# One layer of a hybrid decoder: output weights loaded ahead into other buffers and split by ScalarE and VectorE

## The chip, the cores and the metric

The kernel runs on one core of a Trainium2 chip. The metric is the device time of one execution in microseconds (us). Engines are named as in the profile: PE is TensorE (PEld its weight loads), DVE is VectorE, ACT is ScalarE, POOL is GpSimd, SP is the queue that issues most DMAs.

## The reference, cut to what matters

One layer (1024 positions, width 1024, float32). Both sub-layers have a residual; the lines around the change are:

```
p = modulate(rmsnorm(x)) @ w_in               # q, k, v (512 each) and u (512)
o_attn = stick_breaking(q, k, v)              # 8 heads of 64, in blocks of 128 queries
o_ssm  = s5(u)                                # state-space groups
o = concat([rmsnorm(o_attn, attn_out_g), rmsnorm(o_ssm, ssm_out_g)])
x = x + g1 * (o @ w_out)                      # g1 comes from c @ ada_w
x = x + g2 * ((gelu(gate) * val) @ w_down)    # val, gate: conv of modulate(rmsnorm(x)) @ w_up
```

In stick-breaking attention the weight of key s for query t is sigmoid(z) times the product of (1 - sigmoid(z)) over the keys between s and t, which the kernel forms by a scan along the keys.

## The kernel before

**Precision.** A float32 operand of a large matmul is split in two parts, hi (a rounded copy) and lo (raw minus hi), and each product is three matmuls: hi x hi, hi x lo, lo x hi.

**Stages.** After the norm, the state-space branch and the q and k projections comes the V projection (`proj` with chunk 2): eight tiles of 24 matmuls, three PSUM buffers; ACT and DVE turn each tile into `vt`, which SP writes to DRAM. Then come eight heads. For each tile of 128 queries `head` does: scores `z` on PE, two sigmoids on ACT (`nb`, `sig`), a scan over `nb` on DVE (line 736), a product on POOL into `sig` (line 738), transposes `wT` on PE, their split into `wh` (ACT) and `wl` (DVE), the products `ops` with the values on PE, and their sum into `oT`. Heads 0 to 5 run one after the other. Heads 6 and 7 run together, by groups of 256 queries from the last group (g = 3) to the first, and behind each group `tail_stats` takes the norm of `oT`.

**Output projection.** `w_out` is in eight blocks of 128 rows, k = 0 to 3 for attention (kind 0), 4 to 7 for the state-space half (kind 1). `wout_tile` (line 761) loads one block (`woraw`), scales it by the norm's gain and g1 in place on DVE (`stt`, line 766), rounds it on POOL (`wohi`) and subtracts on POOL (`wolo`). `woraw` has one buffer, tag `x1`, the same in which `ssm_out` accumulates a row tile. `wohi` and `wolo` have four buffers each, so attention's blocks take those of the state-space half. `ssm_out` loads a row tile of x, adds the state-space half's projection (`out_proj`, 24 matmuls `wops`) and writes it to DRAM (`x1_d`). `load_xacc` (line 859) brings those tiles back, two pairs into the `qkraw` buffers and four tiles into one buffer `xs`; `tail_proj` adds attention's half to them (24 matmuls a tile) and starts the second norm (transposes `tp`, line 986).

**Order.** `fillers` is a generator with 58 steps, and `marks` says at which share of the attention work each step is recorded; `ada_fill` does the same for the modulation rows (`ada_raw`, `adps`). A scheduler then fixes the order of instructions on each engine, and each engine runs its queue in that order. `act_copy` is a copy on ACT (line 174), `tt`, `ts` and `stt` are the helpers of lines 60 to 67, `pool_round` that of line 176.

Of the kernel before, what the change touches and what calls it, by code (L numbers as in the profile page):

```python
# [9 lines left out]
F32 = mybir.dt.float32  # L10
# [25 lines left out]
def hybrid_layer_kernel(  # L36
# [17 lines left out]
    act, dve, pool, pe, sp = nc.scalar, nc.vector, nc.gpsimd, nc.tensor, nc.sync  # L54

    def alloc(name, side="left", bufs=1, space=None):
        kw = {} if space is None else {"space": space}
        return tc.alloc_tile_pool(name=name, bufs=bufs, side=side, reuse_waits="tile", **kw)

    def tt(eng, out, a, b, op):  # L60
        eng.tensor_tensor(out=out, in0=a, in1=b, op=op)  # L61
# [4 lines left out]
    def stt(out, a, s, b, op0, op1):  # L66
        dve.scalar_tensor_tensor(out=out, in0=a, scalar=s, in1=b, op0=op0, op1=op1)  # L67

    MUL, ADD, SUB = ALU.mult, ALU.add, ALU.subtract
# [103 lines left out]
    def act_copy(o, i):  # L173
        act.activation(out=o, in_=i, func=AF.Copy)  # L174

    def pool_round(o, i):
        pool.tensor_scalar(out=o, in0=i, scalar1=1.0, scalar2=0.0, op0=MUL, op1=ADD)  # L177
# [37 lines left out]
    for k in range(NK):  # L215
# [4 lines left out]
        raw = ada_raw[k]  # L220
# [10 lines left out]
        hi = wp.tile([128, 512], F32R, tag="whi", name="wu_hi", bufs=8)  # L231
        lo = wp.tile([128, 512], F32R, tag="wlo", name="wu_lo", bufs=8)
# [165 lines left out]
    for i, (tab, k0) in enumerate(((rot[0], 0), (rot[1], 4))):  # L398
        pool.memset(tab[:, 0, :, 0:1], 1.0)
        pool.memset(tab[:, 1, :, 0:1], 0.0)  # L400
        for k in range(4 - i):
            n = 1 << k
# [218 lines left out]
    for cix in range(2):  # L621
        his, los = load_wchunk(cix)
        for tq in range(4):
# [14 lines left out]
            for j in range(2):  # L638
                t = tq * 2 + j
# [12 lines left out]
                for r in range(2):  # L652
                    act.dma_start(out=qk_d[cix, r].rearrange("(a p) t -> p a t", p=128)[:, :, t * 128:(t + 1) * 128],
                                 in_=hl[:, r].bitcast(F32).rearrange("p (a t) -> p a t", t=128))
    smb.release()
    sm.release()
    xq = alloc("qkraw", side="right")
    us = alloc("ffnmix", side="right")
    qp = alloc("qk", side="right")
    xs = alloc("ossm", side="right")  # L660

    def head_load_qk(hd):
        q1, q2, k1 = [qp.tile([128, 1024], F32R, tag=n_, name=n_, bufs=2) for n_ in ("q1", "q2", "k1")]
        for dst, w, sw in ((q1, 0, 0), (k1, 1, 0), (q2, 0, 1)):
            for r in range(2):
                sp.dma_start(out=dst[r * 64:r * 64 + 64].bitcast(F32), in_=qk_d[w, r ^ sw, hd * 64:hd * 64 + 64, :])
        return q1, q2, k1
# [21 lines left out]
    osp = alloc("oprep", side="right", bufs=2)  # L689
# [8 lines left out]
    def head_load_v(hd):  # L698
        vt = ap_.tile([128, 8, 128], F32R, tag="v", name="vsb")
        vload[0] = sp.dma_start(out=vt.bitcast(F32), in_=v_d.rearrange("(t p) h d -> p t h d", p=128)[:, :, hd, :])  # L700
        return vt

    def after_v(f, *a):
        with tc.issue_after(vlast.ins):
            return f(*a)
# [6 lines left out]
    def head(hd, stk, groups, after_tile, after_group):  # L712
        (q1, q2, k1), vt = stk
        pr, h = divmod(hd, 2)
        for g in groups:
# [42 lines left out]
            after_tile(2 * g + 1)  # L758
            after_group(g)

    def wout_tile(kind, kk, his, los):
        k = kind * 4 + kk
        raw = osp.tile([128, 1024], F32, tag="x1", name="woraw", bufs=1)
        sp.dma_start(out=raw, in_=w_out[k * 128:(k + 1) * 128, :])
        yield
        stt(raw, raw, outg_sb[:, k:k + 1], g1row, MUL, MUL)
        yield
        hi = wo.tile([128, 1024], F32R, tag="wohi", name="wohi", bufs=4)
        lo = wo.tile([128, 1024], F32R, tag="wolo", name="wolo", bufs=4)
        pool_round(hi, raw)  # L770
        tt(pool, lo, raw, hi.bitcast(F32), SUB)
        his.append(hi)
        los.append(lo)
        yield
# [40 lines left out]
    def run_all(gen):  # L815
        for _ in gen:
            pass

    psB_new = lambda nm: psM.tile([128, 512], F32, tag="mm", name=nm, bufs=MB)
    oS = xs.tile([128, 4, 8, 128], F32, tag="oS", name="oS")  # L820

    def ssm_stats(inv):
        after_v(lambda: sp.dma_start(out=oS, in_=o_d.rearrange("(k p) j c -> p k j c", p=128)))
        yield
        yield from mix_scale(ap_, psB_new("nps"), oS, range(NT), True, inv)
        yield

    def ssm_out(t, his, los, inv):
        xt_ = osp.tile([128, 1024], F32, tag="x1", name="x1", bufs=1)
        sp.dma_start(out=xt_, in_=x[t * 128:(t + 1) * 128, :])  # L830
        yield from out_proj(osp, psB_new, oS, t, True, his, los, xt_, inv)
        sp.dma_start(out=x1_d[t * 128:(t + 1) * 128, :], in_=xt_)

    def fillers():
        his, los = [], []
        inv = small.tile([128, NT], F32, tag="sinv", name="sinv", bufs=1)
        yield from wout_tile(1, 0, his, los)
        yield from wout_tile(1, 1, his, los)
        yield from ssm_stats(inv)
        yield from wout_tile(1, 2, his, los)  # L840
        yield from wout_tile(1, 3, his, los)
        for t in range(NT):
            yield from ssm_out(t, his, los, inv[:, t:t + 1])
        for kk in range(4):
            yield from wout_tile(0, kk, wa_hi, wa_lo)


    marks = [a + (b - a) * j / n for a, b, n in ((0.02, 0.13, 22), (0.13, 0.68, 24), (0.68, 0.75, 12)) for j in range(n)]
    wa_hi, wa_lo = [], []
    ada_fill = ada_back(ap_, ("adaw", "adacc", 2), psB_new, (c32b, mean32b), range(2, 8))  # L850
    ada_marks = [0.04 + 0.62 * j / 25 for j in range(25)]
    here = [None]
    fill = fillers()
    state = {"q": 0, "w": 0}

    n2inv = small.tile([128, NT], F32, tag="n2inv", name="n2inv", bufs=1)
    xacc = {}

    def load_xacc():
        for i in range(2):  # L860
            t_ = xq.tile([128, 2, 1024], F32, tag="qkraw", name=f"xq{i}", bufs=2)
            for j in range(2):
                xacc[2 - 2 * i + j] = t_[:, j, :]
        t_ = xs.tile([128, 4, 1024], F32, tag="oS", name="xs")
        for j in range(4):
            xacc[4 + j] = t_[:, j, :]
        for t in (6, 7, 4, 5, 2, 3, 0, 1):
            sp.dma_start(out=xacc[t], in_=x1_d[t * 128:(t + 1) * 128, :])

    tail = []  # L870
# [23 lines left out]
    for hd in range(NH):  # L894
        nxt = {}
        last_head = hd >= NH - 2

        def after_tile(i):
            if not last_head:
                if i == 0:  # L900
                    nxt["p"] = (after_v(head_load_qk, 1) if hd == 0 else head_load_qk(hd + 1), head_load_v(hd + 1))
            state["w"] += i + 2
            while ada_marks and ada_marks[0] <= state["w"] / (44.0 * NH):
                ada_marks.pop(0)
                with tc.issue_after(here[0].ins):
                    next(ada_fill, None)
            while state["q"] < len(marks) and marks[state["q"]] <= state["w"] / (44.0 * NH):
                state["q"] += 1
                with tc.issue_after(here[0].ins):
                    next(fill, None)  # L910

        if last_head:
            run_all(fill)
            run_all(ada_fill)
            load_xacc()
            stk2 = (head_load_qk(hd + 1), head_load_v(hd + 1))
            for g in (3, 2, 1, 0):
                head(hd, stk, (g,), after_tile, lambda g: None)
                head(hd + 1, stk2, (g,), after_tile, tail_stats)
            break  # L920
        head(hd, stk, range(4), after_tile, lambda g: None)
        stk = nxt.get("p")
# [280 lines left out]
    for n in range(2):  # L1203
# [15 lines left out]
        for t in range(NT):  # L1219
# [5 lines left out]
            t_ = dx.tile([128, 512], F32, tag="tmp", name="tmp", bufs=2)  # L1225
# [74 lines left out]
```

## Time and profile before

| | |
|---|---|
| median of three timed runs | 1316.16 us (1314.06 to 1320.03) |
| profiled execution | 1318.42 us, span 1316.6 us |
| PE busy, DVE busy | 1224.6 us (93%), 938.2 us (71%) |
| ACT busy, POOL busy | 600.9 us (46%), 460.1 us (35%) |
| mean granted clock of PE | 0.964 |

Times of single rows are us from the span's start. In the table of windows the figure of an engine is its busy time in that window, and `PEclk` the granted clock as a share of full speed. A wait names the instruction that waited, and behind the arrow what ended the wait. In a chain each row is a start, a duration and the work that the next row waited for.

### The profile page before, as it was taken

The page shows a single profiled execution, that of the slowest core. Times are in us where ns is not written, and L with a number is a line of the kernel's source. Part 1 is how long each engine was busy: PE and PEld are TensorE (multiplying, and loading weights), DVE is VectorE, ACT ScalarE, POOL GpSimd, SP SyncE. Part 2 cuts the span into 40 slices and gives each one's busy share as a digit, 9 for nine tenths or more (in the row PEclk, how much of TensorE's full clock was granted, in tenths as well). Part 3 has the DMA queues.
Part 4 walks back from the last instruction along what each step waited for, and adds up shares of the span by engine and source line. Part 5 has one row for each costly group of instructions (what it writes and reads, how often), then busy time and mean ns, then how long its engine had stood idle before and what let it go on. Part 6 is the DMA issues. An engine that isn't in the chain of part 4 may idle for free.

```text
span 1316.6 us, 17819 instructions
## 1 busy us (share of the span) xinstructions
PE 1224.6 (93%) x6384; PEld 994.2 (76%) x6384; DVE 938.2 (71%) x1443; ACT 600.9 (46%) x1039; POOL 460.1 (35%) x363
## 2 busy tenths in 40 slices
PE   5879989998889998769999999999999999999998
PEld 3668868886677767647877888888888888888887
DVE  4867788644897678858888888888888883345334
ACT  6431332423756566435664545545544553223220
POOL 4562370513763334540025545554554510000000
PEclk9988989999879998879999999999999999999999
DMA  9333454628757877214212222222222155447442
GB/s 382 143 84 95 113 167 99 144 89 254 211 144 209 256 195 191 96 64 137 72 48 89 73 96 81 88 72 96 73 80 89 65 191 185 144 168 248 150 137 105
DMA packets 147927, 178.43 MB, mean 136 GB/s; under 512 B 36208, under 2 KB 101888, under 8 KB 146816
## 3 DMA queue, kind: packets, MB, share of 16 engines
q1 hardware_dynamic: 127776, 157.38, 38.5%
q10 hardware_dynamic: 20064, 19.93, 4.4%
q8 instruction: 50, 0.82, 0.3%
q14 instruction: 37, 0.30, 0.1%
HBM read 135.19 MB, written 40.90 MB: 134 GB/s over the span
## 4 chain that ended last, share of the span: by engine, by line
PE 75%; DVE 12%; DMA 8%; issue 2%; ACT 1%; POOL 1%; SPq 0%; ACTq 0%; DVEq 0%; POOLq 0%
PE dnps L1209 6%; PE dnps L1210 6%; PE dnps L1211 6%; PE up_a L1031 6%; PE up_a L1032 6%; PE up_a L1030 6%; PE up_c L1032 3%; PE up_c L1031 3%; PE up_c L1030 3%; DMA ada_raw<-in_ada_r_dram 3%; PE qkvp L563 2%; PE qkvp L561 2%; PE qkvp L562 2%; PE wops L809 2%; PE wops L810 2%
## 5 line engine op out<-in xcount | busy, mean ns | idle before, releaser
L67 DVE SCALAR_TENSOR_TENSOR cv<-up,cols_sb,cv 128x1023 f32<-128x1023 f32 x88 | 147.5, 1677 | 20.5 <-ACT cv L1134 19.7
L61 DVE TENSOR_TENSOR alo<-araw,ahi 128x1024 fp32r<-128x1024 f32 x44 | 53.9, 1225 | 121.1 <-ACT ahi L174 121.0
L61 POOL TENSOR_TENSOR S<-upraw 128x512 f32<-128x512 f32 x40 | 76.0, 1901 | 181.5 <-DVE uplo L61 89.7
L1210 PE MATMUL dnps<-wdlo,ahi 128*128 128x512 f32 x352 | 136.9, 389 | 0.0
L1211 PE MATMUL dnps<-wdhi,alo 128*128 128x512 f32 x352 | 136.9, 389 | 0.0
L1209 PE MATMUL dnps<-wdhi,ahi 128*128 128x512 f32 x352 | 134.7, 389 | 0.0
L61 POOL TENSOR_TENSOR sig<-sig,nb 128x127 f32<-128x127 f32 (+3 forms) x64 | 91.4, 1437 | 97.3 <-DVE nb L736 52.8
L61 DVE TENSOR_TENSOR uplo<-S,uphi 128x512 fp32r<-128x512 f32 x80 | 97.2, 1216 | 27.7 <-ACT uphi L174 27.7
L174 ACT ACTIVATE ahi<-araw 128x1024 fp32r<-128x1024 f32 x44 | 46.6, 1060 | 148.5 <-PE dnps L1210 126.5
L736 DVE TENSOR_TENSOR_SCAN nb<-nb 128x128 f32<-128x128 f32 (+3 forms) x64 | 101.4, 1594 | 11.3 <-ACT nb L734 10.7
L61 POOL TENSOR_TENSOR cv<-cv 128x1024 f32<-128x1024 f32 x22 | 53.4, 2427 | 108.1 <-ACT cv L1138 96.9
L174 ACT ACTIVATE uphi<-S 128x512 fp32r<-128x512 f32 x80 | 49.8, 624 | 81.8 <-POOL S L61 67.6
L562 PE MATMUL qkvp<-w_lo,hhi 128*128 128x512 f32 x192 | 77.1, 402 | 0.0
L561 PE MATMUL qkvp<-w_hi,hhi 128*128 128x512 f32 x192 | 76.6, 402 | 0.0
L1211 PEld LDWEIGHTS dnps<-wdhi,alo 128*128 128x128 f32 x352 | 66.1, 188 | 13.8
L1209 PEld LDWEIGHTS dnps<-wdhi,ahi 128*128 128x128 f32 x352 | 66.1, 188 | 13.8
L1210 PEld LDWEIGHTS dnps<-wdlo,ahi 128*128 128x128 f32 x352 | 66.1, 188 | 13.6
L563 PE MATMUL qkvp<-w_hi,hlo 128*128 128x512 f32 x192 | 76.3, 399 | 0.0
L174 ACT ACTIVATE uphi<-upraw 128x512 fp32r<-128x512 f32 x68 | 42.9, 631 | 66.1 <-POOL cv L61 31.1
L61 DVE TENSOR_TENSOR uplo<-upraw,uphi 128x512 fp32r<-128x512 f32 x68 | 67.7, 996 | 1.5 <-ACT uphi L174 1.5
L1134 ACT ACTIVATE cv<-up,cols_sb 128x1024 f32<-128x1024 f32 x44 | 54.7, 1244 | 11.2 <-DVE up L61 10.4
L809 PE MATMUL wops<-wohi,ohi 128*128 128x512 f32 x128 | 53.4, 422 | 5.8 <-POOL wohi L177 3.8
(334 smaller groups left out, 3401.5 us busy)
## 6 DMA issues: line engine op xcount, KB each, us to landing
upraw<-in_w_up_dram SPq DMA_DIRECT2D x88, 256.0 KB, 3.4
araw<-a_d SPq DMA_DIRECT2D x44, 512.0 KB, 3.3
ada_raw<-in_ada_r_dram SPq DMA_DIRECT2D x64, 256.0 KB, 4.7
a_d<-cv ACTq DMA_DIRECT2D x22, 512.0 KB, 2.8
wdraw<-in_w_down_dram SPq DMA_DIRECT2D x44, 256.0 KB, 4.0
ada_raw<-in_ada_a_dram SPq DMA_DIRECT2D x8, 1024.0 KB, 6.0
qk_d<-hl ACTq DMA_DIRECT2D x32, 256.0 KB, 2.4
q<-qk_d SPq DMA_DIRECT2D x32, 256.0 KB, 7.0
```

What stands on the lines that cost most here:

```text
L61: eng.tensor_tensor(out=out, in0=a, in1=b, op=op)
L67: dve.scalar_tensor_tensor(out=out, in0=a, scalar=s, in1=b, op0=op0, op1=op1)
L174: act.activation(out=o, in_=i, func=AF.Copy)
L561: pe.matmul(o, lhsT=lh, rhs=his[k], start=(k == 0), stop=False)
L562: pe.matmul(o, lhsT=lh, rhs=los[k], start=False, stop=False)
L563: pe.matmul(o, lhsT=ll, rhs=his[k], start=False, stop=(k == NK - 1))
L1030: pe.matmul(ps, lhsT=hi[:, kt, :], rhs=rh, start=(first and kt == 0), stop=False, skip_group_check=True)
L1031: pe.matmul(ps, lhsT=hi[:, kt, :], rhs=rl, start=False, stop=False, skip_group_check=True)
L1032: pe.matmul(ps, lhsT=lo[:, kt, :], rhs=rh, start=False, stop=(kt == 3), skip_group_check=True)
L1209: pe.matmul(o[t], lhsT=hi[:, a], rhs=whi, start=(m == 0), stop=False)
L1210: pe.matmul(o[t], lhsT=hi[:, a], rhs=wlo, start=False, stop=False)
L1211: pe.matmul(o[t], lhsT=lo[:, a], rhs=whi, start=False, stop=(m == NM - 1))
```

## The change

1. Raw output weights no longer lie in the `x1` buffer. Two blocks at a time are loaded by one DMA of 1 MB into a `qkraw` buffer, of which there are two.
2. All eight blocks are rounded by ACT and subtracted by DVE.
3. Attention's four blocks are loaded and scaled among the first four tiles of `ssm_out`, and split behind the last.
4. The marks of the fillers are spread differently: the first 22 steps up to a share of 0.20 (before 0.13), the next 32 up to 0.70, the last 4 up to 0.74.
5. The two pairs of row tiles that come back into the `qkraw` buffers are loaded behind group 3 of head 6, the other four at the start of heads 6 and 7, behind the loads of head 7.

```diff
+    woraw = {}
     def wout_tile(kind, kk, his, los):
         k = kind * 4 + kk
-        raw = osp.tile([128, 1024], F32, tag="x1", name="woraw", bufs=1)
-        sp.dma_start(out=raw, in_=w_out[k * 128:(k + 1) * 128, :])
+        if kk % 2 == 0:
+            woraw[k // 2] = xq.tile([128, 2, 1024], F32, tag="qkraw", name="woraw", bufs=2)
+            sp.dma_start(out=woraw[k // 2], in_=w_out[k * 128:(k + 2) * 128, :].rearrange("(j p) n -> p j n", p=128))
+        raw = woraw[k // 2][:, kk % 2, :]
         yield
         stt(raw, raw, outg_sb[:, k:k + 1], g1row, MUL, MUL)
         yield
...
-        pool_round(hi, raw)
-        tt(pool, lo, raw, hi.bitcast(F32), SUB)
+        act_copy(hi, raw)
+        tt(dve, lo, raw, hi.bitcast(F32), SUB)
...
+        ahead = [wout_tile(0, kk, wa_hi, wa_lo) for kk in range(4)]
         for t in range(NT):
             yield from ssm_out(t, his, los, inv[:, t:t + 1])
-        for kk in range(4):
-            yield from wout_tile(0, kk, wa_hi, wa_lo)
+            if t < 4:
+                for _ in range(2):
+                    next(ahead[t])
+                    yield
+        for w_ in ahead:
+            yield from w_
-    marks = [... ((0.02, 0.13, 22), (0.13, 0.68, 24), (0.68, 0.75, 12)) ...]
+    marks = [... ((0.02, 0.20, 22), (0.20, 0.70, 32), (0.70, 0.74, 4)) ...]
...
-    def load_xacc():
-        for i in range(2):
+    def load_xacc(late_):
+        for i in range(2 * late_):
...
-            load_xacc()
             stk2 = (head_load_qk(hd + 1), head_load_v(hd + 1))
+            load_xacc(False)
             for g in (3, 2, 1, 0):
                 head(hd, stk, (g,), after_tile, lambda g: None)
+                if g == 3:
+                    load_xacc(True)
                 head(hd + 1, stk2, (g,), after_tile, tail_stats)
```

DVE's queue at the V projection, before (`vt` are the V subtractions, `nb` the scans of the first head):

```order
L61 TENSOR_TENSOR hl<-qkT,hl 128x512
L61 TENSOR_TENSOR vt<-qkvp,vt 128x8x64 x7
L693 COPY c32b<-c_sb 128x256
L61 TENSOR_TENSOR vt<-qkvp,vt 128x8x64
L736 SCALAR_TENSOR_TENSOR nb<-nb 128x128
L67 SCALAR_TENSOR_TENSOR woraw<-woraw,cols_sb,g1row 128x1024
L736 SCALAR_TENSOR_TENSOR nb<-nb 128x256
```

The same place now, up to the four subtractions in the first head:

```order
L61 TENSOR_TENSOR vt<-qkvp,vt 128x8x64
L67 SCALAR_TENSOR_TENSOR woraw<-woraw,cols_sb,g1row 128x1024 x4
L61 TENSOR_TENSOR vt<-qkvp,vt 128x8x64 x6
L693 COPY c32b<-c_sb 128x256
L61 TENSOR_TENSOR vt<-qkvp,vt 128x8x64
L736 SCALAR_TENSOR_TENSOR nb<-nb 128x128
L736 SCALAR_TENSOR_TENSOR nb<-nb 128x256
L736 SCALAR_TENSOR_TENSOR nb<-nb 128x384
L736 SCALAR_TENSOR_TENSOR nb<-nb 128x512
L61 TENSOR_TENSOR wl<-wT,wh 128x128
L61 TENSOR_TENSOR wl<-wT,wh 128x2x128
L61 TENSOR_TENSOR wolo<-woraw,wohi 128x1024 x4
```

The four scalings of the state-space half stand behind the first V subtraction, and the four new subtractions before the fifth scan.

PE's queue at the end of attention, before. `ops_6202` are the last products of head 7, `wops_5838` and `wops_5852` the two halves of the first output tile, and the numbers of `wohi` and `wolo` tell the blocks apart (5430 the third, 5437 the fourth):

```order
L743 MATMUL wT_6197<-ident_66,sig_6187 128x128 x2
L753 MATMUL ops_6202<-wh_6169,vsb_5461 128x256
L754 MATMUL ops_6202<-wl_6170,vsb_5461 128x256
L753 MATMUL ops_6202<-wh_6169,vsb_5461 128x256
L754 MATMUL ops_6202<-wl_6170,vsb_5461 128x256
L809 MATMUL wops_5838<-wohi_5430,ohi_5834 128x512
L809 MATMUL wops_5852<-wohi_5430,ohi_5834 128x512
L810 MATMUL wops_5838<-wolo_5431,ohi_5834 128x512
L811 MATMUL wops_5838<-wohi_5430,olo_5835 128x512
L810 MATMUL wops_5852<-wolo_5431,ohi_5834 128x512
L811 MATMUL wops_5852<-wohi_5430,olo_5835 128x512
L809 MATMUL wops_5838<-wohi_5437,ohi_5834 128x512
```

The same place now (the last transposes of the heads, then the first output tile, `wops_5830`, block by block):

```order
L743 MATMUL wT_6148<-ident_66,sig_6138 128x128 x2
L743 MATMUL wT_6175<-ident_66,sig_6165 128x128
L743 MATMUL wT_6189<-ident_66,sig_6179 128x128 x2
L795 MATMUL nps_5799<-ones_71,otot_5802 128x1
L813 MATMUL wops_5830<-wohi_5334,ohi_5826 128x512
L814 MATMUL wops_5830<-wolo_5335,ohi_5826 128x512
L815 MATMUL wops_5830<-wohi_5334,olo_5827 128x512
L813 MATMUL wops_5830<-wohi_5372,ohi_5826 128x512
L814 MATMUL wops_5830<-wolo_5373,ohi_5826 128x512
```

Before, the first output tile was taken apart by blocks and the third and fourth stood behind all work of the heads; now its matmuls stand together, with the last 16 products of the heads between the output tiles.

DVE's queue before the last two heads, now (`x_5224` is the last row tile of `ssm_out`, `nb` are scans of heads 6 and 7):

```order
L736 SCALAR_TENSOR_TENSOR nb<-nb 128x1024
L67 SCALAR_TENSOR_TENSOR x_5224<-wops,sinv,x_5224 128x512
L61 TENSOR_TENSOR wolo<-woraw,wohi 128x1024
L67 SCALAR_TENSOR_TENSOR x_5224<-wops,sinv,x_5224 128x512
L61 TENSOR_TENSOR wolo<-woraw,wohi 128x1024 x3
L61 TENSOR_TENSOR oT<-ops,otmp 64x256
L61 TENSOR_TENSOR wl<-wT,wh 128x4x128
```

Before, no subtraction of an output weight stood on DVE; attention's four scalings stood in the last groups of heads 6 and 7 and behind them.

## Rows read from the trace of the kernel before

**Rows 1.** The page, part 1: busy time, share of the span, instructions.
```profile
PE   1224.6 (93%) x6384; PEld 994.2 (76%) x6384; DVE 938.2 (71%) x1443; ACT 600.9 (46%) x1039; POOL 460.1 (35%) x363
```

**Rows 2.** Windows: PE, PEld, DVE, ACT, POOL busy, PEclk, DMA share, GB/s.
```profile
316.00:340.00 24.00, 16.32 (x71) 12.38 (x72) 18.63 (x21) 15.13 (x38) 19.79 (x10) 0.74 1.04 298
340.00:390.00 50.00, 41.67 (x292) 34.86 (x292) 48.46 (x62) 37.07 (x77) 35.37 (x37) 0.82 0.56 150
390.00:540.00 150.00, 136.26 (x1042) 109.33 (x1040) 111.64 (x164) 88.18 (x207) 52.16 (x67) 0.97 0.72 201
...
550.00:560.00 10.00, 6.24 (x27) 5.27 (x28) 9.79 (x19) 2.29 (x5) 9.04 (x10) 0.50 0.15 52
...
567.00:575.00 8.00, 5.39 (x31) 4.16 (x29) 7.66 (x24) 3.51 (x9) 3.23 (x5) 1.00 0.19 66
575.00:588.00 13.00, 6.25 (x15) 3.54 (x15) 2.08 (x4) 0.38 (x1) 6.70 (x4) 0.56 0.23 82
588.00:635.00 47.00, 44.93 (x209) 36.47 (x208) 36.87 (x105) 27.89 (x52) 0.00 (x0) 0.98 0.42 146
```

**Rows 3.** Waits in 566 to 590 us: total, times, longest.
```profile
POOL wohi L177 <- DVE woraw L67: 9.4, 2, 4.8
DVE woraw L67 <- DMA woraw<-in_w_out_dram: 4.9, 1, 4.9
```

**Rows 4.** Chain of waits, 570 to 600 us: start, duration, work.
```profile
573.63 1.21 DVE woraw L67
...
576.04 2.36 POOL wolo L61
578.42 3.06 DMA woraw<-in_w_out_dram
581.62 1.30 DVE woraw L67
...
584.12 2.36 POOL wolo L61
...
591.16 0.23 PE wops L810
```

**Rows 5.** Groups by line, PE, 568 to 635 us.
```profile
L810 PE MATMUL wops<-wolo,ohi 128*128 128x512 f32 x63 | 26.1, 415 | 2.8 <-POOL wolo L61 2.8
```

**Rows 6.** Costliest groups of the page, and the tile woraw (ns min/median/max).
```profile
L61 DVE TENSOR_TENSOR alo<-araw,ahi 128x1024 fp32r<-128x1024 f32 x44 | 53.9, 1225 | 121.1 <-ACT ahi L174 121.0
L174 ACT ACTIVATE ahi<-araw 128x1024 fp32r<-128x1024 f32 x44 | 46.6, 1060 | 148.5 <-PE dnps L1210 126.5
...
L177 POOL TENSOR_SCALAR wohi<-woraw x8: 1042/1050/2475, 325.7 to 583.0; 128x1024 fp32r<-128x1024 f32 x8
L61 POOL TENSOR_TENSOR wolo<-woraw,wohi x8: 2349/2881/4183, 329.4 to 584.1; 128x1024 fp32r<-128x1024 f32 x8
```

**Rows 7.** Groups on DVE, 316 to 340 us; timeline of DVE and POOL, 545 to 556.
```profile
L736 DVE TENSOR_TENSOR_SCAN nb<-nb 128x384 f32<-128x384 f32 x1 | 0.9, 933 | 0.0
...
552.02 1.94 DVE L736 TENSOR_TENSOR_SCAN nb<-nb 128x384 f32<-128x384 f32 x1
...
549.87 3.27 POOL L61 TENSOR_TENSOR wolo<-woraw,wohi 128x1024 fp32r<-128x1024 f32 x1
```

**Rows 8.** Timeline of the V projection; DMA issues of the page (KB, us to landing).
```profile
284.29 1.30 DVE L61 TENSOR_TENSOR gt<-gps,spar 128x512 f32<-128x512 f32 x2 [3.51 <-PE gps L532]
286.58 0.68 DVE L61 TENSOR_TENSOR vt<-qkvp,vt 128x512 fp32r<-128x512 f32 x1
289.94 0.69 DVE L61 TENSOR_TENSOR vt<-qkvp,vt 128x512 fp32r<-128x512 f32 x1 [2.69 <-ACT vt L675]
...
ada_raw<-in_ada_a_dram SPq DMA_DIRECT2D x8, 1024.0 KB, 6.0
```

**Rows 9.** Timeline of PE: transposes at full and at half clock.
```profile
538.78 0.81 PE L743 MATMUL wT<-ident,sig 128*128 128x128 f32 x6
...
559.76 1.70 PE L743 MATMUL wT<-ident,sig 128*128 128x128 f32 x7
```

More of the change, by code (lines that the diff above doesn't have):

```diff
@@ L841, in fillers @@
         yield from wout_tile(1, 3, his, los)
+        ahead = [wout_tile(0, kk, wa_hi, wa_lo) for kk in range(4)]
         for t in range(NT):
             yield from ssm_out(t, his, los, inv[:, t:t + 1])
-        for kk in range(4):
-            yield from wout_tile(0, kk, wa_hi, wa_lo)
-    marks = [a + (b - a) * j / n for a, b, n in ((0.02, 0.13, 22), (0.13, 0.68, 24), (0.68, 0.75, 12)) for j in range(n)]
+            if t < 4:
[4 more added lines that the diff above has]
+            yield from w_
+    marks = [a + (b - a) * j / n for a, b, n in ((0.02, 0.20, 22), (0.20, 0.70, 32), (0.70, 0.74, 4)) for j in range(n)]
     wa_hi, wa_lo = [], []
@@ L863, in load_xacc @@
                 xacc[2 - 2 * i + j] = t_[:, j, :]
[L864 to L867, printed above, removed]
+        if not late_:
+            t_ = xs.tile([128, 4, 1024], F32, tag="oS", name="xs")
+            for j in range(4):
+                xacc[4 + j] = t_[:, j, :]
+        for t in ((2, 3, 0, 1) if late_ else (6, 7, 4, 5)):
             sp.dma_start(out=xacc[t], in_=x1_d[t * 128:(t + 1) * 128, :])
```

## The prediction

> **What bounds the kernel now.** I read the page first. TensorE (PE) is busy for 93% of the span [rows 1], so time is lost only where it stands still, or where its granted clock falls from 2.4 to 1.2 GHz. The table of windows shows where that is [rows 2]. The change touches nothing outside attention and the step behind it, so four stretches matter:
>
> - 316 to 390 us, the first heads: PE is busy for 58 of 74 us. VectorE (DVE) is full from 340 on (48.46 of 50), GpSimd (POOL) before that (19.79 of 24).
> - 390 to 540 us, heads and SSM output projections side by side: PE is busy for 136.26 of 150, DVE for 111.64.
> - 550 to 560 us, the last heads: DVE is full (9.79 of 10), PE has 6.24 at a granted clock of 0.50.
> - 567 to 588 us: PE has 5.39 of 8 and then 6.25 of 13 at 0.56, and DVE only 2.08 in the second part. Nobody is full: this is a chain.
>
> The waits name the chain: POOL waits 9.4 us for the scaled weights, and DVE 4.9 us for their DMA [rows 3]. The chain of waits gives it in order of time [rows 4]: the third attention weight is scaled (573.63) and split on POOL (until 578.4), only then is the one buffer free and the fourth load starts (578.42), then scaling (581.62) and the split again (584.12). PE's queue holds the output projection of the first tile, which needs the fourth weight, ahead of all else. From 588 on PE is full to 635.
>
> **Part 1: the end of attention.** The new order puts all eight scalings and splits ahead of the last two heads, so that chain goes. What PE then has to do stays. From 568 to 635 it issues 188 of the 192 projection matmuls (62, 63 and 63 on three lines, one of them in [rows 5]); at 0.23 us each [rows 4] that is 43 us, beside transposes and the last heads' products. Lost are 8 - 5.39 = 2.6 us in 567 to 575; in 575 to 588 the 6.25 busy us at 0.56 are worth 3.5, so 9.5 are lost. Together 12 us. What is late next is the statistics of the last tiles, a string of short DVE operations that so far ran in the hole and now must run beside the matmuls. DVE has 36.87 busy of 47 us in 588 to 635, so it has room for some 10 us of them. Bounds: 14 us if the 2.1 us without PE in 588 to 635 go too, 8 us if 4 us of the statistics come out in the open. I take -12.
>
> **Part 2: the V projection.** This cost is one that the diff does not tell, and the order does. The first four raw weights now come in two loads of 1 MB, issued ahead of the V rows, and DVE's queue has all four scalings between its first and its second V subtraction. Behind them on DVE stand seven V subtractions; each frees one of the three PSUM tiles of the projection, and PE needs them. The buffers lie in the memory of the state-space tables, whose last reader on DVE ends at 284.29 + 1.30 = 285.6 [rows 8]. A 1 MB load takes 6.0 us to land [rows 8], so the first is there at 292 and the second between 292 and 298. Four scalings at 1.21 to 1.30 us [rows 4] are 5 us, so the second V subtraction moves from 289.94 [rows 8] to 297 to 300. Eight tiles of 24 matmuls at 0.23 us run at 5.5 us each and the projection ends just before 316; the fifth tile, which waits for the second subtraction, would start about 293. PE then stands for 4.5 to 8 us. If 1 MB lands in 4 us it is 3; if the two loads hinder each other, 9. Nothing else is ready for PE, and the first head stands behind it. I take +6.
>
> **Part 3: splits from POOL to ScalarE (ACT) and DVE.** Eight roundings go to ACT at 1.06 us [rows 6], 8.5 us on an engine with 46% load: I take nothing, since PE and DVE are the engines that fill up, and 8.5 us if that cover is gone. Eight subtractions go to DVE at 1.225 us [rows 6]: 9.8 us. Six of the old pairs ran among the heads, two in the hole. POOL loses eight pairs of at least 1.04 + 2.35 us [rows 6], among the heads 20 us. Scalings: four leave the first heads for the V projection and four come there from the end, two of which stood among full DVE work, so DVE has 2.5 us more there.
>
> What POOL's part is worth shows in [rows 7]: a 384-column scan took 0.933 us early on, and 1.94 us when it started at 552.02 beside a POOL subtraction (549.87, 3.27 us long). It ended 0.85 us after that subtraction, about its own length: it had waited for POOL. The Trainium skill, SBUF — State Buffer, "SBUF: two separate sides", says that DVE with two SBUF inputs and a GpSimd operation that reads SBUF lock each other out of a shared port pair for a whole instruction. That scan agrees. The rule also holds for the new DVE subtractions against POOL's products, which speaks against the change; by it the trade is 20 us of POOL for 9.8 us of DVE, a gain of 10 us.
>
> Bounds from rows: +7 us if nothing comes back from POOL and 9.8 - 2.55 of DVE's new work is in the open (the subtractions against the scalings that DVE loses from its full stretches); -12 us if 20 us of POOL had held DVE and its products in full, against 7.3 to 9.8. The early stretch was POOL's, the middle PE's (DVE has 38 us free there, so half of the new work can hide), the end DVE's. Between far ends I take -4, on the side of the one scan that was measured.
>
> **Part 4: fillers spread wider.** All projection and modulation work is still there and still ends before the last two heads, somewhat earlier in the order. I take 0: PE was at 91% in the middle. Bounds: -3 and +5, the first if fill moves into the 16 idle us of the first heads, the second if the last heads, with less between them, run at 1.2 GHz for part of the way.
>
> **Sum.** -12 + 6 - 4 + 0 = -10 us against the profiled execution, 1318.42 us: 1308.4. The median of the three timed runs is 2.3 us lower, 1316.16, so I forecast 1306.
>
> **Rivals.**
> - More gain, 1297: the weights land in time for the V projection (+3) and POOL's relief is the full one (-10): -12 + 3 - 10 = -19. For it: the scan in [rows 7], and POOL full in 316 to 340. Against it: four DVE subtractions stand in a row in the first head, before the fifth scan, so part of the early gain is spent at once.
> - No gain, 1318: DVE takes the whole new work and becomes the bound among the heads (+7), the V projection loses 7: -12 + 7 + 7 = +2. For it: DVE is at 97% in 340 to 390. Against it: 38 us of DVE idle time in 390 to 540.
> - Slower, 1324: TensorE's clock in the last two heads. Without fillers PE has pauses there, as in 550 to 560, where the clock was 0.50 [rows 2]. Six transposes took 0.81 us at full clock and seven 1.70 us at half [rows 9]. The last two heads hold some 80 transposes, 80 products and 60 score matmuls, an estimated 30 us at full clock from such rows and 60 at half, where DVE needs about 54. So PE is 6 us over DVE, the first 24 projection matmuls cost 24 x 0.23 = 5.5 more, and PE's longer steps within each tile's chain to the scan an estimated 6: +18 on my sum. It decides if the clock stays down for the whole 50 us; if it is down for under 20, DVE hides it. The Trainium skill, TensorE: Matmul & The Clock Gate, "What's actually happening", says the gate is throttled by default and only activity opens it; the 0.50 of 550 to 560, behind a stretch with PE half busy, agrees.
>
> **How the numbers follow.** Forecast 0.47 (own range 1299 to 1313), more gain 0.24, no gain 0.15, slower 0.14. Within 0.5% (6.6 us, about what a measurement here can tell from no change) means 1309.6 to 1322.7. Faster takes the second case and three quarters of the first: 0.24 + 0.36 = 0.60. Same takes a quarter of the first and 0.12 of the third: 0.23. Slower has the rest, 0.17. The range is 1292 to 1321: the lower end is 14 + 9 - 3 = 20 us of gain and a little more, the upper one leaves out most of the slower case.
>
> **What would show it.** Right: no POOL work on output weights; PE without a hole between the last transposes of the heads and the first norm transposes, where 67 us become about 55; a V subtraction on DVE that waits for weights, and PE idle for some 6 us before the first score matmul; scans of the first heads nearer to their short times. Wrong: PE still waits for a split weight late (Part 1 fails); the first scores come at 316 as before (Part 2); scans as long as before and DVE at 97% throughout (Part 3); a granted clock of 0.5 through both last heads (the slower case).

## The result and the profile after

The changed kernel takes 1306.67 us (median of 4 runs, 1304.25 to 1308.42) against 1315.53 us of the kernel before (four runs, with the three that gave 1316.16): a ratio of 0.9925, 95% interval 0.9903 to 0.9948. Timed again beside other kernels it has 1308.47 us and 0.9936 (0.9914 to 0.9958). So it is faster, by some 8 to 9 us; 1306 was forecast. The profiled execution took 1306.83 us, its span is 1305.1 us.

Part 1 of the page of the changed kernel, to be read against [rows 1]: POOL has 38 us less, DVE 8 and ACT 6 more, and PE the same work.

```profile
PE 1221.6 (94%) x6384; PEld 991.0 (76%) x6384; DVE 946.5 (73%) x1451; ACT 606.8 (46%) x1047; POOL 421.9 (32%) x347
```

The windows of [rows 2] in the changed kernel (PE, PEld, DVE, ACT and POOL busy, PEclk, DMA share, GB/s):

```profile
316.00:340.00 24.00, 17.86 (x94) 13.39 (x93) 16.92 (x20) 14.83 (x34) 9.17 (x13) 0.79 0.91 260
340.00:390.00 50.00, 39.72 (x289) 30.55 (x288) 48.06 (x66) 37.29 (x80) 21.51 (x26) 0.86 0.72 196
390.00:540.00 150.00, 136.62 (x1012) 109.44 (x1011) 118.31 (x160) 91.67 (x213) 50.87 (x67) 0.95 0.71 202
550.00:560.00 10.00, 7.87 (x48) 6.64 (x47) 9.94 (x13) 7.62 (x18) 4.76 (x8) 0.84 0.01 2
567.00:575.00 8.00, 7.01 (x40) 5.80 (x41) 6.42 (x17) 2.82 (x8) 1.05 (x4) 1.00 0.00 0
575.00:588.00 13.00, 12.14 (x59) 9.92 (x57) 9.57 (x28) 5.97 (x11) 0.00 (x0) 1.00 0.21 82
```

The hole at 575 to 588 is filled (12.14 us of PE at full clock, before 6.25 at 0.56), and DVE has 9.57 us of work in it, statistics and sums of the last tiles (before 2.08). No wait of POOL or DVE for a weight is left there: the scalings that [rows 3, 4] showed late are done by 361 us, the last split by 530.

What it costs stands earlier. The V projection in the changed kernel, as the timeline has it (start, duration; in brackets the idle time before, and what ended it). DVE:

```profile
285.22 0.68 DVE L61 TENSOR_TENSOR vt<-qkvp,vt 128x512 fp32r<-128x512 f32 x1
289.63 2.61 DVE L67 SCALAR_TENSOR_TENSOR woraw<-woraw,cols_sb,g1row 128x1024 f32<-128x1024 f32 x2 [3.73 <-DMA woraw<-in_w_out_dram]
293.11 2.48 DVE L67 SCALAR_TENSOR_TENSOR woraw<-woraw,cols_sb,g1row 128x1024 f32<-128x1024 f32 x2 [0.87 <-DMA woraw<-in_w_out_dram]
296.53 1.29 DVE L61 TENSOR_TENSOR vt<-qkvp,vt 128x512 fp32r<-128x512 f32 x2 [0.94 <-ACT vt L675]
```

ACT:

```profile
285.33 0.37 ACTq L653 DMA_DIRECT2D qk_d<-hl  x1
286.38 1.06 ACT L536 ACTIVATE gt<-gt 128x1024 f32<-128x1024 f32 x1
295.90 1.09 ACT L675 ACTIVATE vt<-qkvp 128x512 fp32r<-128x512 f32 x2 [8.46 <-DMA o_d<-gt]
```

The same copy in the kernel before:

```profile
286.69 0.37 ACTq L653 DMA_DIRECT2D qk_d<-hl  x1
289.31 0.60 ACT L675 ACTIVATE vt<-qkvp 128x512 fp32r<-128x512 f32 x1 [0.51 <-DMA qk_d<-hl]
```

PE of the changed kernel:

```profile
291.35 0.39 PE L563 MATMUL qkvp<-w_hi,hlo 128*128 128x512 f32 x1
297.37 0.77 PE L561 MATMUL qkvp<-w_hi,hhi 128*128 128x512 f32 x1 [5.63 <-DVE vt L61]
...
300.92 0.63 PE L563 MATMUL qkvp<-w_hi,hlo 128*128 128x512 f32 x1
301.34 0.49 PE L561 MATMUL qkvp<-w_hi,hhi 128*128 128x512 f32 x1
301.68 0.39 PE L562 MATMUL qkvp<-w_lo,hhi 128*128 128x512 f32 x1
```

The second V subtraction starts at 296.53 instead of 289.94 [rows 8], and PE stands for 5.63 us. The scalings hold DVE until 295.59 (293.11 + 2.48). What ended its last 0.94 us of waiting is not a scaling: it is ACT's copy of the same tile, which itself waited 8.46 us for a DMA (0.51 before). The profile names the stores of the state-space output (`o_d`) for it; the experiments say more. After the pause the matmuls follow each other every 0.43 us until 301.34 (half clock), and then every 0.23.

Three marks cut the kernel where the change acts: the first score matmul, the start of the last scan, and the last projection matmul. "Heads" is the time between the first two, "end" between the last two, each from one profiled execution. Ratios are to the kernel before, timed beside each on the same chip.

| kernel | median us | ratio (95%) | first score | last scan | last projection | heads | end |
|---|---|---|---|---|---|---|---|
| before | 1315.5 | 1 | 316.2 | 566.3 | 634.6 | 250.1 | 68.2 |
| changed | 1306.7 | 0.9925 (0.9903-0.9948) | 322.8 | 568.2 | 623.0 | 245.4 | 54.8 |
| changed, again (e9) | 1308.5 | 0.9936 (0.9914-0.9958) | 324.6 | 574.0 | 628.7 | 249.4 | 54.7 |
| e1 scalings spread | 1312.8 | 0.9978 (0.9963-0.9993) | 321.9 | 572.8 | 627.6 | 250.9 | 54.8 |
| e2 splits on POOL | 1322.4 | 1.0040 (1.0019-1.0061) | 322.3 | 580.9 | 635.7 | 258.6 | 54.8 |
| e3 old marks | 1313.6 | 0.9991 (0.9975-1.0007) | 322.6 | 575.2 | 630.0 | 252.6 | 54.7 |
| e4 before, splits moved | 1319.2 | 1.0025 (1.0006-1.0045) | 314.2 | 565.9 | 632.1 | 251.7 | 66.2 |
| e5 loads behind V | 1314.2 | 0.9981 (0.9957-1.0005) | 315.2 | 577.1 | 631.9 | 261.9 | 54.8 |
| e6 attention weights recorded late | 1309.8 | 0.9953 (0.9934-0.9972) | 322.8 | 570.0 | 624.9 | 247.2 | 54.9 |
| e7 order shifted (marks) | 1314.3 | 0.9990 (0.9973-1.0006) | 322.7 | 576.4 | 631.1 | 253.7 | 54.7 |
| e8 half the splits on POOL | 1318.2 | 1.0013 (0.9994-1.0032) | 323.8 | 576.1 | 630.9 | 252.3 | 54.8 |
| e10 order shifted (modulation) | 1314.0 | 0.9973 (0.9955-0.9990) | 322.6 | 575.4 | 630.1 | 252.8 | 54.7 |
| e11 loads among V stores | 1307.7 | 0.9930 (0.9906-0.9955) | 317.9 | 572.6 | 627.3 | 254.7 | 54.7 |
| e12 the same and e6 | 1299.3 | 0.9868 (0.9837-0.9898) | 317.6 | 566.4 | 621.1 | 248.8 | 54.8 |

The table is read by columns. "End" has two values: 66 to 68 with one raw buffer, 54.7 to 54.9 with two pairs, whatever else was done. "First score" follows the loads. "Heads" scatters over 245 to 262. Between the two runs of the very same kernel it differs by 4 us, so a difference of heads below that says nothing in a single profile, and medians are compared instead. The profiled executions of e9, e11 and e12 are the slowest of their runs (1313.8, 1311.0 and 1305.8 us), so their marks lie late.

### The profile page after: what moved, and what is told of

Same layout as the page of the kernel before. It is cut to its first block, busy times and chain, and to the rows that moved or that the text cites. A ratio compares the mean times of both kernels' runs of the same rounds, so it can differ in the third digit from the quotient of the medians.

```text
span 1305.1 us, 17833 instructions
## 1 busy us (share of the span) xinstructions
PE 1221.6 (94%) x6384; PEld 991.0 (76%) x6384; DVE 946.5 (73%) x1451; ACT 606.8 (46%) x1047; POOL 421.9 (32%) x347
## 4 chain that ended last, share of the span: by engine, by line
PE 73%; DVE 14%; DMA 6%; ACT 2%; issue 2%; POOL 1%; SPq 1%; ACTq 0%; DVEq 0%; POOLq 0%
PE dnps L1222 6%; PE dnps L1221 6%; PE dnps L1223 6%; PE up_a L1043 6%; PE up_a L1044 6%; PE up_a L1042 6%; PE up_c L1043 3%; PE up_c L1044 3%; PE up_c L1042 3%; PE qkvp L561 2%; PE qkvp L563 2%; PE qkvp L562 2%; DVE nb L736 2%; PE wops L813 2%; DMA ada_raw<-in_ada_r_dram 2%
## 5 line engine op out<-in xcount | busy, mean ns | idle before, releaser
L736 DVE TENSOR_TENSOR_SCAN nb<-nb 128x128 f32<-128x128 f32 (+3 forms) x64 | 96.6, 1521 | 7.2 <-ACT nb L734 6.8
L734 ACT ACTIVATE nb<-z 128x512 f32<-128x512 f32 (+2 forms) x96 | 48.5, 506 | 29.4 <-PE z L733 18.4
L1146 ACT ACTIVATE cv<-up,cols_sb 128x1024 f32<-128x1024 f32 x44 | 54.7, 1244 | 11.2 <-DVE up L61 10.4
```

The source lines that it names most:

```text
L736: dve.tensor_tensor_scan(out=nb[:, 0:n][:, ::-1], data0=nb[:, 0:n][:, ::-1], data1=nb[:, 0:n][:, ::-1], initial=1.0, op0=MUL, op1=ALU.bypass)
```

## The experiments

**e1, spread scalings.** Undoes the order on DVE that Part 2 of the prediction blamed.

```diff
+        with tc.issue_after(vsub[kk + 1 if kind else 7].ins):   # vsub: the V subtractions
             stt(raw, raw, outg_sb[:, k:k + 1], g1row, MUL, MUL)
```

> The changed kernel, but the scalings of the four state-space weights may not be issued before V subtractions 2, 3, 4 and 5 (one each), so that none stands between the first and the second. Theory (the V stall of 5.6 us on PE is a loss of its own, paid in full): the wait of PE for the V subtractions goes, the first score matmul comes at 316 us instead of 322.8, all behind it moves up by as much, and the time falls by 5 to 7 us to 1300 to 1302, a ratio to the kernel before of about 0.988. Rival (the first heads are limited by VectorE, and what the scalings cost ahead of them they cost anyway): the first scores come at 316 but the last scan still starts near 568, and the time stays within 1.5 us of 1306.7, a ratio of about 0.9925.

Neither came true. No scaling stands between the first two V subtractions any more, and PE waits as long as before (5.8 us). ACT in the timeline of this kernel:

```profile
284.24 0.37 ACTq L653 DMA_DIRECT2D qk_d<-hl  x1
294.93 1.09 ACT L676 ACTIVATE vt<-qkvp 128x512 fp32r<-128x512 f32 x2 [8.58 <-DMA o_d<-gt]
```

PE's wait (total, times, longest us):

```profile
PE qkvp L561 <- DVE vt L677: 5.8, 1, 5.8
```

Its DMA issues between 278 and 303 us (KB each, median us from issue to landing):

```profile
woraw<-in_w_out_dram SPq DMA_DIRECT2D x2, 1024.0 KB
qk_d<-hl ACTq DMA_DIRECT2D x3, 256.0 KB, 10.6
```

So DVE's order is not needed for the stall. The V copy shares two staging buffers (`hl`, `vt`) with the last transposed keys, and may not start before these are stored. Only one of the three stores in this view has a landing time, the one issued at 284.24: it landed 10.6 us later, at 294.85, and the copy started at 294.93. It was this store that held the copy, then, and not the `o_d` stores that the profile names; they do not read these buffers. Before, the copy waited 0.51 us for the same store. The theory for the next runs was that the two 1 MB loads, issued just ahead, hold it up.

**e2, splits back on POOL.**

```diff
-        act_copy(hi, raw)
-        tt(dve, lo, raw, hi.bitcast(F32), SUB)
+        pool_round(hi, raw)
+        tt(pool, lo, raw, hi.bitcast(F32), SUB)
```

> The changed kernel with all eight splits (rounding and subtraction) back on GpSimd, buffers, order of the loads and filler marks as changed. Theory (taking 20 us from GpSimd is worth 4 to 5 us between the first score and the last scan, because VectorE no longer waits for the shared port): scans get longer again (mean 1.52 to about 1.59 us), the last scan starts 4 to 5 us later than at 568.2, the end behind it keeps its 54 to 55 us, 1310 to 1312, ratio about 0.996. Rival 1 (the gain among the heads came from the spread fillers): scans longer, but the time within 1.5 us of 1306.7. Rival 2 (VectorE is the limit and 9.8 us of subtractions on it were in the way): 1300 to 1303.

The direction is that of the theory, the size is larger: 1322.4 us, some 14 more than the changed kernel (and some 8 more than e7 and e10 below, which are the changed kernel in a slightly different order). DVE at the start of the last two heads:

```profile
539.54 3.82 DVE L736 TENSOR_TENSOR_SCAN nb<-nb 128x1024 f32<-128x1024 f32 x1
543.28 0.39 DVE L61 TENSOR_TENSOR oT<-ops,otmp 64x256 f32<-64x256 f32 x1
543.60 7.01 DVE L736 TENSOR_TENSOR_SCAN nb<-nb 128x640 f32<-128x640 f32 x2
```

POOL in the same stretch:

```profile
537.13 8.39 POOL L61 TENSOR_TENSOR wolo<-woraw,wohi 128x1024 fp32r<-128x1024 f32 x2
545.76 3.23 POOL L61 TENSOR_TENSOR wolo<-woraw,wohi 128x1024 fp32r<-128x1024 f32 x1
548.96 7.63 POOL L61 TENSOR_TENSOR sig<-sig,nb 128x895 f32<-128x895 f32 x3
```

PE's longest wait there:

```profile
PE wT L743 <- POOL sig L61: 7.0, 1, 7.0
```

The row of 7.01 us holds a scan of 640 columns (3.27 us) and one of 768 (3.82), whose shortest times in this trace are 1.47 and 1.75. The three POOL subtractions beside the scans took 4.08, 4.34 and 3.23 us (2.349 at best, [rows 6]). They end in turn, POOL at 541.21, DVE at 543.36, POOL at 545.51, DVE at 546.87, POOL at 548.99, DVE at 550.61: from one end to the next it is about the time that the next one takes alone. So DVE and POOL hold each other up. The Trainium skill, SBUF — State Buffer, "SBUF: two separate sides", describes such a lock between a DVE instruction with two inputs in SBUF and a GpSimd instruction that reads SBUF; these rows agree with it.

There is a second cost that the lock alone does not give: POOL's products of the scans, which PE needs, queue behind all four splits, and PE stands 7.0 us for one of them. In the first two heads, where the four state-space splits stand, e2 takes 62.2 us from the first score to the second head's last scan, and the changed kernel 55.6.

**e3, old marks.**

```diff
-    ((0.02, 0.20, 22), (0.20, 0.70, 32), (0.70, 0.74, 4))
+    ((0.02, 0.13, 22), (0.13, 0.68, 24), (0.68, 0.75, 12))
```

> The changed kernel with the filler marks of the kernel before (22 up to 0.13, 24 up to 0.68, 12 up to 0.75), so that the state-space projections and the first steps of the attention weights come earlier and closer together at the start. Theory (the marks are worth nothing): within 2 us of 1306.7, ratio 0.991 to 0.994. Rival (the 4.7 us that the heads got shorter are the marks): 1310 to 1312, ratio about 0.996, with the last scan 4 to 5 us later than 568.2 and TensorE slower in 340 to 540.

It looks like the rival (1313.6 us, last scan 7 us later). The seventh and tenth experiments take that reading away: orders that differ much less lose as much.

**e4, the splits alone on the kernel before** (the edit of e2 the other way round, one raw buffer).

> The kernel before with one part of the change alone: the splits on ScalarE and VectorE instead of GpSimd; one raw buffer, the old order and the old marks. Theory (GpSimd relief is worth 4 to 5 us among the heads; in the hole at the end two rounds of 3.3 us on GpSimd become two of 2.3): 1309 to 1312, ratio 0.995 to 0.997, the hole at 575 to 588 still there. Rival (VectorE is the limit among the heads and takes the new work in full): 1315 to 1322, ratio 1.000 to 1.005.

The rival's side: 1319.2 us, ratio 1.0025 (1.0006 to 1.0045). The end is shorter by 2 us, as the sum of the shorter splits said, but the heads gain nothing (251.7 against 250.1; the first two heads 49.5 against 50.3), and the hole stays:

```profile
575.00:588.00 13.00, 7.62 (x21) 4.70 (x22) 8.24 (x19) 4.10 (x7) 0.00 (x0) 0.74 0.26 90
```

(The window as above, of this kernel: PE 7.62 of 13 us at 0.74.) With one raw buffer the splits come one at a time (they start at 322.8, 348.3, 366.0 and 378.7 us in the first heads), and there no worth of POOL's relief shows. That it has one when four splits come together fits e2, but a new order may cost as much as e4 lost (e7, e10), so this is likely and not shown.

**e5, loads behind V.**

```diff
-            sp.dma_start(out=woraw[k // 2], ...)
+            after_v(lambda: sp.dma_start(out=woraw[k // 2], ...))
```

> The changed kernel, but the two 1 MB loads of the state-space weights are issued behind the last store of V on the SP queue, not ahead of these stores. Theory, new after the first four runs (the V stall comes from the loads, not from the scalings: ScalarE may not copy the second V tile before its staging buffer's store has landed, and that store shares the DMA engines with 2 MB of weights): PE's wait of 5.6 us for V goes, the first score matmul is at 316 instead of 322.8; the four scalings move into the first heads and cost there up to 5 us of VectorE, so the time is 1300 to 1306 (within the scatter that a new order brings). Rival (the eight stores of the state-space output hold the staging buffers, the loads do not matter): the wait stays at 5 to 6 us, first scores at 322.

The stall is gone and the first scores come at 315.2. ACT of this kernel:

```profile
286.69 1.06 ACT L536 ACTIVATE gt<-gt 128x1024 f32<-128x1024 f32 x1
288.29 0.60 ACT L675 ACTIVATE vt<-qkvp 128x512 fp32r<-128x512 f32 x1 [0.54 <-DMA qk_d<-hl]
289.59 0.60 ACT L675 ACTIVATE vt<-qkvp 128x512 fp32r<-128x512 f32 x1 [0.71 <-DMA v_d<-vt]
```

The second copy waits 0.54 us instead of 8.46, for the store of the keys. With e1 this settles what held ACT's copy: the loads ahead, not the scalings. It does not clear the scalings: loaded early and left in their place they would by themselves hold DVE until 295.59, only 0.94 us before the subtraction started, and e5 moves them out of the way too. By these rows, an estimate, either of the two makes most of the stall by itself, so that taking one away shows little; no run has the scalings alone. The Trainium skill, DMA: Bandwidth & Descriptors, "Issuing engines are not separate DMA queues", says that DMAs issued by different engines run on the same 16 DMA engines and interleave; a store from ACT's queue that takes 10.6 us beside loads from SP's (e1) agrees with it.

But the total does not gain: 1314.2 us, against 1300 to 1306 expected, since the heads take 261.9 us. They do not lose it at once. Counted from the first score, the second head's last scan starts after 57.0 us (55.6 in the changed kernel), the sixth head's after 186.6 (187.7). But the weights are split later (342 to 365 us instead of 328 to 334), the state-space projections start at 403.6 instead of 387.9, and filler work is left over: 81 projection and 72 modulation matmuls stand behind the sixth head's last scan, where the changed kernel has 36 and 14. From there to the last scan it takes 75 us instead of 58. How much of that loss is order, no run separates.

**e6, attention weights recorded late.**

```diff
-            if t < 4:
-                for _ in range(2):
-                    next(ahead[t])
-                    yield
```

> The changed kernel with the first two steps of each attention weight taken out from between the state-space projections, so that all four attention weights are loaded, scaled and split in one go after the eighth projection; two raw buffers as changed. Theory (it is the second raw buffer pair and not the early start that removes the hole at the end): the end from the last scan to the last projection matmul keeps 54 to 55 us, last two heads 57 to 61 us, time within 5 us of 1306.7. Rival (the early start is needed): the last load is late for the last two heads, PE waits for weights again, the end is 58 us or more, time over 1312.

The numbers are the theory's: end 54.9, 1309.8 us. But the edit did not make the weights late. DVE's scalings of the four attention weights in this kernel:

```profile
348.61 2.46 DVE L67 SCALAR_TENSOR_TENSOR woraw<-woraw,cols_sb,g1row 128x1024 f32<-128x1024 f32 x2
357.20 3.85 DVE L67 SCALAR_TENSOR_TENSOR woraw<-woraw,cols_sb,g1row 128x1024 f32<-128x1024 f32 x2
```

In the changed kernel:

```profile
348.63 2.47 DVE L67 SCALAR_TENSOR_TENSOR woraw<-woraw,cols_sb,g1row 128x1024 f32<-128x1024 f32 x2
357.23 3.84 DVE L67 SCALAR_TENSOR_TENSOR woraw<-woraw,cols_sb,g1row 128x1024 f32<-128x1024 f32 x2
```

The scheduler still issues both loads (334.3 and 336.5 us) and the scalings as early as in the changed kernel. In both that is ahead of the first state-space projection matmul (387.9 us), not among its tiles, as the change was described; only the four splits moved, and they moved ahead (507.8 to 514 us instead of 523.9 to 530). So whether the early start is needed was not tested. What stands is that every kernel with two raw buffer pairs has the end of 54.7 to 54.9 us, with the old marks too (e3), and with its last split as late as 555 us (e5); with one buffer the last split ends at 586.5 [rows 4] and the end is 68.2.

**e7 and e10, the same work in a slightly different order.**

```diff
-    ((0.02, 0.20, 22), (0.20, 0.70, 32), (0.70, 0.74, 4))     # e7
+    ((0.02, 0.20, 22), (0.20, 0.69, 32), (0.69, 0.74, 4))
-    ada_marks = [0.04 + 0.62 * j / 25 for j in range(25)]     # e10
+    ada_marks = [0.04 + 0.61 * j / 25 for j in range(25)]
```

> The changed kernel with one filler mark boundary at 0.69 instead of 0.70: no operation added, removed or moved between engines; only the order in which the same instructions stand changes a little. Theory (the order alone is worth several us, and the gain of 4.7 us among the heads that I put down to GpSimd is partly that): between 1303 and 1312, at least 2 us away from 1306.7, with the difference between first score and last scan. Rival (order scatter is small, and the losses of the first and third experiment belong to their edits): within 1.5 us of 1306.7, ratio 0.991 to 0.994.

> The changed kernel with the last mark of the modulation fillers at 0.65 instead of 0.66 of the attention work: no operation added, removed or moved between engines, a slightly different order. Theory (the end is fixed by the two buffer pairs; the heads scatter with the order, 245 us in the changed kernel being the short end): last scan to last projection matmul 54 to 55 us, first score to last scan between 246 and 256, time 1306 to 1316. Rival (the changed kernel's heads are the rule and the shift in the seventh experiment was special): 245 +-1.5 us and 1305 to 1308.

Both lose 5 to 8 us in the median, by which of the two runs of the changed kernel is taken, with nothing added or taken away; e7 by more than its theory allowed (1312). e10 shows where: up to about 480 us DVE and PE have the changed kernel's order, and the traces run level. Two windows of the changed kernel:

```profile
440.00:480.00 40.00, 32.20 (x237) 24.47 (x236) 28.01 (x38) 19.25 (x49) 15.85 (x19) 0.91 0.73 189
480.00:568.00 88.00, 76.58 (x492) 63.69 (x491) 75.22 (x101) 58.34 (x130) 35.16 (x43) 0.90 0.48 149
```

The same two of e10:

```profile
440.00:480.00 40.00, 32.35 (x239) 24.60 (x238) 28.10 (x38) 19.37 (x49) 15.86 (x19) 0.91 0.73 189
480.00:568.00 88.00, 71.47 (x452) 57.92 (x450) 69.57 (x83) 52.88 (x116) 33.56 (x35) 0.88 0.49 151
```

In the first window they are alike; in the second, which ends where the changed kernel's last scan starts, e10 has got 5 us less done on PE and 6 on DVE. (In the second profile of the changed kernel PE has 75.49 us there and DVE 72.73, so 1 us of PE's difference and half of DVE's is chance.) That is order alone, and it is most of the whole gain of the change: with either of these orders the same change is worth 1 to 4 us (ratios 0.9990 and 0.9973).

**e8, half the splits on POOL** (the state-space four; attention's stay on ACT and DVE).

> The changed kernel with the four state-space splits on GpSimd and the four attention splits on ScalarE and VectorE. Theory (the loss of the second experiment came from four GpSimd subtractions in the last two heads, where two 640-column scans took 7.0 us beside one): first heads as there, last two heads 57 to 60 us instead of 64, time 1304 to 1311. Rival (GpSimd work costs the same wherever it stands): half the loss of the second experiment, 1313 to 1316.

The median sides with the rival, and even beyond it: 1318.2 us. The last two heads do take 58.9 us instead of 64.3, as the theory had it, but the first two are late. The second head's last scan starts at 386.7 us here and at 384.5 in e2, against 377.4 to 380.2 in the seven profiles with the same loads and splits on ACT and DVE (changed, e1, e3, e6, e7, e9, e10). Counted from the first score that is 62.9 and 62.2 us, against 55.1 to 56.8 in the seven. So POOL costs some 5 to 8 us among the first heads, outside the scatter of these orders. The 5 us between e2 and e8 in the last two heads stand on one profile each.

**e9, the changed kernel again.**

> The changed kernel itself once more, as the measure for the other kernels. Both theories: a ratio of 0.990 to 0.995 as the first time, time 1304 to 1309; last scan at 568, last projection matmul at 623.

The ratio came as expected. The profiled execution was the slowest of its ten (1313.78 us), which is why its marks lie 2 and 6 us late.

**e11 and e12, loads among the V stores.**

```diff
+            with tc.issue_after(vst[2 + kk if kind else 7].ins):    # vst: the V stores
                 sp.dma_start(out=woraw[k // 2], ...)
...
+        with tc.issue_after(vsub[kk + 4 if kind else 7].ins):
             stt(raw, raw, outg_sb[:, k:k + 1], g1row, MUL, MUL)
```

> The changed kernel with the two 1 MB loads of state-space weights behind the third and the fifth store of V, and their scalings behind V subtractions 5 to 8. Theory (only the position of the loads ahead of the staging stores makes the V stall): PE's wait for V is under 1 us, first score matmul at 315 to 317, the four scalings done when the heads start, and the time 5 to 7 us under what the same heads would give, 1299 to 1309 with the scatter of the order. Rival (2 MB delay the V stores wherever they stand): PE waits 3 to 6 us for V, only later, first scores at 319 to 322, time 1306 to 1313.

> The loads as in the experiment before, and the attention weights in one go after the eighth state-space projection. Theory: first scores at 315 to 317, the heads between 245 and 256, the end 54 to 55 us, 1299 to 1309. Rival as there: first scores at 319 to 322, 1306 to 1313.

PE no longer stands within the projection, but the last V subtraction is late (PE waits 2.6 and 3.3 us for it, 1.4 before), and the first scores come at 317.9 and 317.6, a little over the theory's 315 to 317. ACT's last two copies of V wait 3.17 us each, by the profile the first of them for a V store and the second for a scaling. So the rival has a part too: a V store beside the loads is late here as well, only at less cost. e11 ends where the changed kernel does, with heads of 254.7 us. e12, with e6's simpler order of the attention weights, takes 1299.3 us, 0.9868 (0.9837 to 0.9898): better than both kernels, and the lowest of all runs. e12 differs from e6 in the place of these loads and scalings alone and is some 11 us faster; e11 differs from the changed kernel in the same and is 1 us faster at most. Since one shift of the order is worth 5 to 8 us, how much of e12's gain is the mended V projection stays open.

## Why the prediction was right

- **Part 1, -12:** 13.4 us measured (end 68.2 to 54.8), in every kernel with two raw buffer pairs. The statistics that were to be late next fit beside the matmuls (DVE 9.57 of 13 us in the old hole), so it came close to the -14 of the bounds. The prediction gave the credit to the order that has all splits ahead of the last two heads; the runs show that it comes with the two buffer pairs, whatever the marks (e3), and not with the new engines of the splits (e4, 66.2). Buffers and early start were not tried apart.
- **Part 2, +6:** the first scores are 6.5 us later. From the first V subtraction on the stage is 7.9 us longer (37.6 against 29.7), 5.6 of them PE's wait and about 2 the half clock behind it, which the sum did not have. The size was right, the mechanism only half. The queue of scalings that it named is there and ended at 295.59. But the wait that ended last is one that it did not have: ACT's copy came at 295.90, held by the store of the keys behind the loads. e1 took the scalings away and changed nothing; e5 took both away and the stage is as long as before (29.7). "If the two loads hinder each other" was in the text, but not that they hinder others. That the two causes end within 1 us of each other, so that the size came out, is luck. Nor is it shown that the total pays these 8 us: e5 and e11 save most of them and are not faster for it.
- **Part 3, -4, and Part 4, 0:** the heads took 4.7 us less, which looks like the -4. It is not shown to be that. The same kernel's second profile has 0.7 less, and e7 and e10 lose 5 to 8 us of the median with neither part touched. The step that failed is the one that priced the POOL relief by itself: on the old buffers no worth shows (e4), with the new ones its lack costs 8 to 14 us (e2), of which 5 to 8 lie in the first two heads whatever the order (e2, e8). The rows of e2 point to the four splits that come together there, ahead of POOL's products, and that is Part 1's doing. So the two parts are likely not a sum. Part 4's own worth lies under the scatter of the order.
- **The sum:** -10 forecast, -8.9 measured. In the profiles the stages give -1.4 ahead of the V projection (chance: +0.2 in e9), +7.9, -4.7 and -13.4, together -11.6. The two large terms were sized well; the small ones agreed by a margin that no run confirms. That the total came so near is partly luck: the same work in the orders of e7 and e10 takes 1314.3 and 1314.0 us, outside the forecast's own 1299 to 1313. The 9 in the lower end of the range, "14 + 9 - 3", does not fit Part 3, whose bound is 12; with it the gain is 23 us, which is 1293.
- **The rivals:** the slower one has some truth. The granted clock in the last heads was 0.66 in 530 to 540 and 0.70 in 540 to 550, but 0.84 and 0.95 in the two stretches after, so not down for the whole 50 us. DVE was full beside it (9.97 of 10 us in 530 to 540, 9.94 in 550 to 560), so it probably hid the slow clock; no run shows that. The "no gain" rival had DVE as the bound: 48.06 of 50 us in 340 to 390 is what it said, but PE got 136.62 us in the middle, as before.

## What to carry to other kernels

A load that is issued early is not free because its own consumer has time: ask which small stores on the same DMA engines free a buffer that the stage in progress waits for, and issue it behind them, but not so late that its own consumer waits (e5). If two waits end close together, taking one away changes nothing (e1): look at what would end the wait next. Look in the trace whether an edit moved what it was to move (e6). Relief of an engine has a price only in a given order, so price edits that feed each other together. Where a scheduler sets the order, shift something harmless once or twice and time it, before a gain of that size is put down to an edit.

## What was not expected of the hardware

- A store of 256 KB from ACT's queue took 10.6 us to land beside 2 MB of loads from SP's (e1; 2.5 us median before, 2.4 in e11). A single 0.5 MB V store and eight small ones of 64 KB stood in the same stretch.
- DVE scans and POOL subtractions stretch one another: a scan of 640 and one of 768 columns 7.01 us together, against 1.47 and 1.75 at best, and 1024-column POOL subtractions up to 4.34 us each, against 2.349 at best [rows 6].
- A pause of 5.63 us of PE is followed by 4 us at half clock (matmuls every 0.43 us from 297.37 to 301.34), so the wait alone understates its cost by about 2 us.
